# Moving the second layer's memory keys and values into the first layer, and three products and norm rows into another order

## The chip, the core and the metric

The kernel runs on one core of a Trainium2 chip. The metric is the device time of one execution in microseconds (us). TensorE (PE) multiplies matrices and loads its stationary operand (PEld) beside that, VectorE (DVE) and ScalarE (ACT) do elementwise work, GpSimd (POOL) does elementwise work and issues some DMAs, SyncE (SP) issues the weight loads.

## What is computed

The reference is a two-layer transformer block (`first_block`) and a second block with sparse attention and retention behind it. 512 tokens, width 1024, all in float32. Only the first block is touched by the change:

```python
mem_n = rmsnorm(mem, mem_norm)
for i in range(DEPTH):                       # DEPTH = 2
    if i == N_A:                             # layer 1 (called B)
        kv = rmsnorm(x, kv_norm) @ w_kv
        k, v = jnp.split(kv, 2, axis=-1)
        ...
    mem_kv = mem_n @ w_mem_kv[i]             # memory keys and values, 256 rows
    mk, mv = jnp.split(mem_kv, 2, axis=-1)
    h = rmsnorm(x, norm_mix[i])
    ...                                      # layer 0 (A): short convolution, layer 1 (B): band attention
    y_mem = _mem_attention(q_mem, mk, mv)
    x = x + jnp.concatenate([y_tok, y_mem], axis=-1) @ w_out
    h = rmsnorm(x, norm_ffn[i])
    x = x + (jax.nn.silu(h @ w_gate[i]) * (h @ w_up[i])) @ w_down[i]
```

The memory rows `mem_n` are the same in both layers; only the weights `w_mem_kv[i]` differ.

## The kernel before

Activations lie transposed: 8 chunks of 128 features by 512 tokens. A float32 product is made of three PE products of rounded parts (high by high, low by high, high by low: lines 120 to 122, or 142 to 144 for token-major results, or 575 to 577 in the feed-forward). A weight unit is 512 KB: SP loads it into `wr` (2 buffers), ACT rounds it to `wh` (line 70), DVE subtracts to get `wl` (line 80; 3 buffers each). One unit of 128 output features feeds 24 products (8 chunks by 3).

The program runs: `load_consts`, `layer_a`, `ffn(0)`, `layer_b`, `ffn(1)`, `second`. The framework fixes the order of each engine's instructions when it builds the program: an engine is given, of the instructions that its estimate holds ready, the one that stands earliest in the program text. Buffers of one tag (`b`, `t`, `s`, `x`, PSUM banks `pp`, `lg`, `tp`, `po`) are given out in text order and come back when the last reader is done. On the chip each engine then runs its list strictly in order.

The places that the change touches:

- `layer_a` (line 479): conv blocks 0 and 1, then `mem_kv(0)`, the memory queries and attention, conv blocks 2 to 5, then `residual`. A conv block is three weight units; its DVE results go through POOL (products `v` and `y`, line 73), then ACT and DVE.
- `mem_rows` (line 350) loads `mem` (1 MB), sums squares, makes the norm of the memory rows (`token_mean` at 174, `rsqrt`, `spread` at 203 to 207 into `mR`), and splits the gained rows into `gm` (8 chunks, tag `v`). `mem_kv` (372) multiplies them: two key units, two value units, 24 products of 256 columns each.
- `run` passes `between` to `ffn(0)`: there, before the last eight down products, `bias_loads`, `mem_kv(1)` (which loads and splits `mem` again) and `bias_tables` (which writes the 2.3 MB band table in DRAM) are called.
- `gate_up` (566): seven block products into the banks U, Y and Z; U is copied out by ACT (`g1`, `g2`, `u`) between its products; `between(0)` and `between(1)` insert down products of the group before. It is used from f = `PLAIN` = 5 on.
- `layer_b` (673): `hk` (8 chunks gained for keys), the norm (`square_sum`, `token_mean`, `rsqrt`, `spread` into `Rb`), `h` (8 chunks gained for queries), saving of x to DRAM (`xres`), then the two key products (`w_kv_k`), the values (`w_kv_v`), memory attention, band attention.

Of the kernel before, what the change touches and what calls it, by code (L numbers as in the profile page):

```python
# [9 lines left out]
F32R = mybir.dt.float32r  # L10
# [15 lines left out]
PLAIN = 5  # L26


class Build:
# [319 lines left out]
    def mem_rows(self):  # L349

        nc, T = self.nc, self.T
        chunks = []
        for i in range(4):
            t = self.slot("q", name="mem").rearrange("p (c n) -> p c n", c=2)
            nc.sync.dma_start(t, T["mem"][:, 2 * i:2 * i + 2])
            chunks += [t[:, 0], t[:, 1]]
        if self.mrs is None:
            acc = self.square_sum(chunks, 256, True, tags=("pa", "pa"))
            self.mrs = self.keep(self.rsqrt(self.token_mean(acc, 256, 1e-5, 1024.0)), "mrs")
            self.mR = self.spread(self.mrs, "mR")  # L360
        g = self.gain(5)
        res = []
        for c, x in enumerate(chunks):
            if c % 2 == 0:
                t = self.slot("v", F32R, (128, KWORDS), "gm")
            hi, lo = (t[:, a:a + 256] for a in (512 * (c % 2), 512 * (c % 2) + 256))
            self.copy(hi, x, g[:, c:c + 1])
            self.lo_of(lo, x, hi, g[:, c:c + 1])
            res.append((hi, lo))
        return res  # L370

    def mem_kv(self, layer):
        nc, T = self.nc, self.T
        gm = self.mem_rows()
        ks = []
        for b in range(2):
            ps = self.psum("lg")[:, :256]
            self.proj(ps, T["w_mem_k"][layer, b], gm)
            kk = self.slot("t", name="mk")[:, :256]
            self.mul(kk, ps, self.mR)  # L380
            ks += self.stack_k(kk, True)
        vs = []

        def done(tb, ps):
            hl = [self.slot("b", F32R, name="mv")[:, :384] for _ in range(2)]
            for t in hl:
                nc.gpsimd.memset(t.bitcast(F32), 0.0)
            hi, lo = (t.rearrange("p (i c) -> p i c", i=2) for t in hl)
            for i in range(2):
                for o in range(2):  # L390
                    src = ps[:, 128 * i + 64 * o:128 * i + 64 * o + 64]
                    d = slice(128 * o, 128 * o + 64)
                    self.copy(hi[:, i, d], src, self.mrs[:, tb:tb + 1])
                    self.lo_of(lo[:, i, d], src, hi[:, i, d], self.mrs[:, tb:tb + 1])
            vs.append(hl)

        self.proj_tok(T["w_mem_v"][layer], gm, 256, 2, done, tag=("tp",) if layer else ("lg",))
        return ks, vs

    def mem_attention(self, qs, ks, vs):  # L400

# [77 lines left out]
    def layer_a(self):  # L479
        nc, T = self.nc, self.T  # L480
        h = self.h0 + self.gained(self.x[1:], self.gain(0)[:, 1:])
        _, R = self.norm_row(1e-5, "Ra", True)
        ys = [self.conv_block(0, h, R, "b", self.w0)]
        ys.append(self.conv_block(1, h, R, "b", banks=("lg", "lg", "po")))
        ks, vs = self.mem_kv(0)
        qs = []
        for b in range(2):
            qs += self.stack_q(self.queries(T["a_w_in"][18 + b], h, R))
        ym = self.mem_attention(qs, ks, vs)
        for c in range(2, 6):  # L490
            ys.append(self.conv_block(c, h, R, "pb"))
        self.residual(T["a_w_out"], ys + ym)

    def halves(self, x, R, gain):
# [68 lines left out]
        put_sum("s4", s2, a12)  # L563
        return res

    def gate_up(self, src, B, between):

        nc, w = self.nc, self.pair_weights(src)
        mm = nc.tensor.matmul
        b11, b21, m1, m2, t3, b22, m4 = B  # L570

        def product(ps, a, b, start):
            for j in range(4):
                (ah, al), (bh, bl) = (a[0][:, j], a[1][:, j]), b[j]
                mm(ps, ah, bh, start=start and j == 0, stop=False, skip_group_check=not start)  # L575
                mm(ps, ah, bl, start=False, stop=False, skip_group_check=not start)  # L576
                mm(ps, al, bh, start=False, stop=j == 3, skip_group_check=not start)  # L577

        U, Y, Z = (self.psum(t)[:, :256] for t in ("pp", "lg", "lg"))
        g, u = self.slot("t", name="g"), self.slot("t", name="u")[:, :256]  # L580
        g1, g2 = g[:, :256], g[:, 256:]
        add = lambda out, a, b: nc.vector.tensor_tensor(out, a, b, op=ALU.add)  # L582
        product(U, w["a11"], b11, True)
        self.copy(g1, U)
        product(Y, w["a12"], b21, True)
        add(g1, Y, g1)
        product(U, w["s2"], m2, False)
        self.copy(g2, U)
        product(Z, w["s1"], m1, True)
        product(U, w["s3"], t3, False)  # L590
        self.copy(u, U)
        add(u, Z, u)
        between(0)
        product(Z, w["s4"], b22, False)
        add(g2, Z, g2)
        nc.scalar.activation(g, g, AF.Silu)  # L596
        product(U, w["a22"], m4, False)
        between(1)
        act = self.slot("t", name="act")
        self.mul(act[:, :256], U, g1)  # L600
        self.mul(act[:, 256:], u, g2)
        return self.split(act, "b", name="act")
# [14 lines left out]
        self.mul(u, u, z, self.nc.gpsimd)  # L617
        return self.split(u, "b", name="act"), R

    def ffn(self, layer, between_last=None):  # L620
        nc, T = self.nc, self.T
        gain = self.gain(2 + layer)
        h = self.gained(self.x, gain)
        R = B = act = None
# [17 lines left out]
        for g, (f0, f1) in enumerate(FFG):  # L642
            last = act
            todo = [] if last is None else [p for i in range(4) for p in down(i, last, g - 1)]
            act = []
            n = f1 - f0
            shares = [0] * n if last is None else [4, 2, 1, 1] if f0 < PLAIN else [8 * (i + 1) // n - 8 * i // n for i in range(n)]
            for f, share in zip(range(f0, f1), shares):
                mine, todo = todo[:share], todo[share:]

                def between(i):
                    for p in mine[i * (len(mine) // 2):] if i else mine[:len(mine) // 2]:
                        p()

                if f < PLAIN:
                    a, R = self.plain_gate_up(layer, f, h, R)
                    if f == 0:
                        steps = self.halves(self.x, R, gain)
                    sets = next(steps, None) or sets
                    between(0)  # L660
                    between(1)
                else:
                    if f == PLAIN:
                        B = [[s[i] for s in sets] for i in range(7)]
                    a = self.gate_up(T["w_gu"][layer, f - PLAIN], B, between)
                act.append(a)
        if between_last:
            between_last()
        for i in range(4):
            for p in down(i, act, len(FFG) - 1):  # L670
                p()
# [1 line left out]
    def layer_b(self):  # L673
        nc, T = self.nc, self.T
        hk = self.gained(self.x, self.gain(4), ["pa"] * 3 + ["pb"] * 5)
        rs, R = self.norm_row(1e-5, "Rb", True)
        rs = self.keep(rs, "rsb")
        h = self.gained(self.x, self.gain(1))
        xd = self.dr.tile([8, 128, 512], F32, name="xres")
        for c in range(8):  # L680
            nc.gpsimd.dma_start(xd[c], self.x[c])
        ks = []
        for b in range(2):
            ps = self.psum("pp")
            self.proj(ps, T["w_kv_k"][b], hk)
            kk = self.slot("t", name="k")
            self.mul(kk, ps, R)
            ks += self.stack_k(kk, tag="x")
        vs = []

        def done(tb, ps):
# [4 lines left out]
                vs.append(self.last_value(ps, rs[:, 3:]))  # L696

        self.proj_tok(T["w_kv_v"], hk, 256, 4, done, tag=("pp", "lg"))
        mk, mv = self.mem1
        qs = []  # L700
        for b in range(2):
            qs += self.stack_q(self.queries(T["b_w_q"][6 + b], h, R))
# [456 lines left out]

    def run(self):  # L1160
        self.load_consts()
        self.mrs = None
        self.layer_a()
        def between():
            loaded = self.bias_loads()
            self.mem1 = self.mem_kv(1)
            self.bias_tables(loaded)

        self.ffn(0, between)
        self.layer_b()  # L1170
        self.ffn(1)
        self.second()
# [123 lines left out]
```

## Time and profile before

| | us |
|---|---|
| median of 3 runs | 1663.72 (1663.45 to 1664.67) |
| the profiled execution | 1665.43 |
| its span, first to last instruction | 1663.6 |
| PE busy in the span | 1617.0 (97%) |
| PEld busy | 1415.1 (85%) |
| DVE busy | 1238.1 (74%) |
| ACT busy | 763.1 (46%) |
| POOL busy | 162.7 (10%) |

The profiled execution took 1.8 us beside its span and 1.7 us more than the median. PE is busy in nearly all of the span, but the end of a product is modelled and products overlap, so that busy time alone does not tell how fast PE runs: the distance from the start of one product to the start of the next does. A row of a timeline gives the start, the duration, the engine, the line, the operation, what it writes and reads, and in brackets how long the engine stood idle before it and what it waited for.

### The profile page before, as it was taken

The numbers are of one execution on the slowest core, as the hardware profiler recorded it, in microseconds if no ns is written. First come the engines' busy times: TensorE is split into PE (matmuls) and PEld (weight loads), VectorE is DVE, ScalarE is ACT, GpSimd is POOL, SyncE is SP. The second block draws the span as 40 slices with busy tenths as digits, with TensorE's granted clock in tenths as the row PEclk, the third lists the DMA queues.
The fourth block names the chain that finished last, engine by engine and source line by source line (L and its number), as shares of the span: only waits on it lengthen the run. The fifth ranks groups of instructions, "written<-read, shape, count | busy, mean of one in ns | idle before, by whom it ended". The sixth has DMA issues, their size and how long they took to land.

```text
span 1663.6 us, 24425 instructions
## 1 busy us (share of the span) xinstructions
PE 1617.0 (97%) x9408; PEld 1415.1 (85%) x9408; DVE 1238.1 (74%) x2342; ACT 763.1 (46%) x1418; POOL 162.7 (10%) x160
## 2 busy tenths in 40 slices
PE   8999999999999899999999999998999999999997
PEld 6887888999998688888899999987888888888887
DVE  7865787778776869978876877698788877764443
ACT  6532254445444557734444444444465533333333
POOL 1112410000000200051000000111001000010010
PEclk9999999999999899999999999999999999999999
DMA  6222223333323532222333333343501122243342
GB/s 201 89 85 93 92 86 101 115 93 94 117 90 118 197 107 64 78 94 76 114 102 98 93 102 104 89 166 98 163 26 58 45 83 83 71 152 115 126 160 88
DMA packets 51573, 171.61 MB, mean 103 GB/s; under 512 B 6680, under 2 KB 6880, under 8 KB 51328
## 3 DMA queue, kind: packets, MB, share of 16 engines
q1 hardware_dynamic: 45504, 151.11, 28.1%
q0 software_dynamic: 5376, 18.82, 3.4%
q8 instruction: 74, 1.21, 0.3%
q14 instruction: 43, 0.35, 0.1%
q10 hardware_dynamic: 576, 0.11, 0.0%
HBM read 160.56 MB, written 11.81 MB: 104 GB/s over the span
## 4 chain that ended last, share of the span: by engine, by line
PE 75%; DVE 12%; DMA 5%; issue 3%; ACT 3%; POOL 1%; SPq 0%; DVEq 0%; ACTq 0%; POOLq 0%
PE pp L122 8%; PE pp L120 8%; PE pp L121 8%; PE lg L120 4%; PE lg L121 4%; PE lg L122 4%; PE pp L575 3%; DMA wr<-in_w_gu_dram 3%; PE pp L576 3%; PE pp L577 3%; PE tp L120 3%; DVE wl L80 3%; PE tp L121 3%; PE tp L122 3%; PE tp L262 2%
## 5 line engine op out<-in xcount | busy, mean ns | idle before, releaser
L70 ACT ACTIVATE wh<-wr 128x1024 fp32r<-128x1024 f32 (+3 forms) x246 | 251.8, 1024 | 353.0 <-PE pp L121 130.3
L80 DVE TENSOR_TENSOR wl<-wr,wh 128x1024 fp32r<-128x1024 f32 (+3 forms) x246 | 305.3, 1242 | 53.8 <-ACT wh L70 52.5
L120 PE MATMUL pp<-g,wh 128*128 128x512 f32 x592 | 234.8, 397 | 8.5 <-ACT wh L70 8.0
L122 PE MATMUL pp<-g,wl 128*128 128x512 f32 x592 | 234.4, 396 | 0.6 <-DVE wl L80 0.6
L121 PE MATMUL pp<-g,wh 128*128 128x512 f32 x592 | 233.5, 394 | 0.0
L120 PEld LDWEIGHTS pp<-g,wh 128*128 128x128 f32 x592 | 112.0, 189 | 30.9 <-ACT wh L70 8.8
L122 PEld LDWEIGHTS pp<-g,wl 128*128 128x128 f32 x592 | 111.7, 189 | 22.6 <-DVE wl L80 1.5
L121 PEld LDWEIGHTS pp<-g,wh 128*128 128x128 f32 x592 | 111.9, 189 | 20.8 <-DVE g L76 0.6
L70 ACT ACTIVATE s<-s 128x512 fp32r<-128x512 f32 x136 | 84.8, 631 | 45.0 <-DVE s L555 42.9
L120 PE MATMUL tp<-acth,wh 128*128 128x512 f32 x264 | 103.8, 393 | 0.5 <-DVE mv L76 0.5
L121 PE MATMUL tp<-actl,wh 128*128 128x512 f32 x264 | 103.5, 392 | 0.0
L122 PE MATMUL tp<-acth,wl 128*128 128x512 f32 x264 | 102.8, 389 | 0.0
L80 DVE TENSOR_TENSOR s<-s,s 128x512 fp32r<-128x512 f32 x136 | 90.5, 684 | 0.3
L575 PE MATMUL pp<-Bh,s 128*128 128x256 f32 x272 | 79.0, 291 | 5.0 <-ACT g L70 4.8
L577 PE MATMUL pp<-Bh,s 128*128 128x256 f32 x272 | 78.0, 287 | 0.0
L575 PE MATMUL lg<-Bh,s 128*128 128x256 f32 x272 | 77.1, 283 | 0.0
L555 DVE TENSOR_TENSOR s<-wr,wr 128x512 f32<-128x512 f32 x68 | 46.8, 688 | 40.6 <-DMA wr<-in_w_gu_dram 40.2
L577 PE MATMUL lg<-Bh,s 128*128 128x256 f32 x272 | 76.9, 283 | 0.0
L596 ACT ACTIVATE g<-g 128x512 f32<-128x512 f32 x34 | 21.5, 632 | 83.3 <-DVE g L582 83.3
L122 PEld LDWEIGHTS tp<-acth,wl 128*128 128x128 f32 x264 | 49.7, 188 | 10.8
L575 PEld LDWEIGHTS pp<-Bh,s 128*128 128x128 f32 x272 | 53.0, 195 | 6.8 <-ACT g L70 6.6
L576 PE MATMUL pp<-Bl,s 128*128 128x256 f32 x204 | 58.5, 287 | 0.0
(503 smaller groups left out, 4546.6 us busy)
## 6 DMA issues: line engine op xcount, KB each, us to landing
wr<-in_w_gu_dram SPq DMA_DIRECT2D x68, 512.0 KB, 3.9
wr<-in_w_in_dram SPq DMA_DIRECT2D x44, 512.0 KB, 3.5
wr<-in_w_down_dram SPq DMA_DIRECT2D x32, 512.0 KB, 3.6
wr<-in_a_w_in_dram SPq DMA_DIRECT2D x18, 512.0 KB, 3.5
wr<-in_w_down_dram SPq DMA_DIRECT2D x16, 384.0 KB, 3.2
wr<-in_w_gate_dram SPq DMA_DIRECT2D x10, 512.0 KB, 3.4
wr<-in_w_up_dram SPq DMA_DIRECT2D x10, 512.0 KB, 3.4
wr<-in_a_w_out_dram SPq DMA_DIRECT2D x8, 512.0 KB, 3.4
```

The lines of the kernel that those rows point to most:

```text
L70: self.nc.scalar.activation(out, in_, AF.Copy, scale=scale)
L80: self.nc.vector.tensor_tensor(out, x, hi.bitcast(F32), op=ALU.subtract)
L120: mm(ps, ah, bh, start=start, stop=False)
L121: mm(ps, ah, bl, start=False, stop=False)
L122: mm(ps, al, bh, start=False, stop=stop)
L262: self.nc.tensor.transpose(ps[:, c:c + 128], src, self.ident)
L555: nc.vector.tensor_tensor(t, a, b, op=ALU.add)
L575: mm(ps, ah, bh, start=start and j == 0, stop=False, skip_group_check=not start)
L576: mm(ps, ah, bl, start=False, stop=False, skip_group_check=not start)
L577: mm(ps, al, bh, start=False, stop=j == 3, skip_group_check=not start)
L596: nc.scalar.activation(g, g, AF.Silu)
```

## The change

`mem_rows` returns the sum of squares; the norm of the memory rows is made in `mem_kv(0)` behind the first key product. `mem_kv(1)` runs in layer A behind conv block 3 from the same `gm`; its keys and values go to DRAM (`set_aside`, 12 stores on the POOL queue) and come back in layer B (`bring_back`, 8 loads on the POOL queue). The band table is made behind conv block 4. In `gate_up` for f = 5 the first inserted down product stands ahead of the `s2` product and no longer behind `u`. In `layer_b` the norm sum stands behind the first key product and the norm row behind the second; `h` and the saving of x follow them.

```diff
-        if self.mrs is None:
-            acc = self.square_sum(chunks, 256, True, tags=("pa", "pa"))
-            self.mrs = self.keep(self.rsqrt(self.token_mean(acc, 256, 1e-5, 1024.0)), "mrs")
-            self.mR = self.spread(self.mrs, "mR")
+        acc = self.square_sum(chunks, 256, True, tags=("pa", "pa"))
...
-    def mem_kv(self, layer):
+    def mem_kv(self, layer, gm, acc=None):
...
             self.proj(ps, T["w_mem_k"][layer, b], gm)
+            if acc is not None and b == 0:
+                self.mrs = self.keep(self.rsqrt(self.token_mean(acc, 256, 1e-5, 1024.0)), "mrs")
+                self.mR = self.spread(self.mrs, "mR")
...
+    def set_aside(self, ks, vs):
+        self.aside = [self.dr.tile([128, n], F32R, name=f"aside{i}") for i, n in enumerate([512] * 4 + [384] * 4)]
+        for d, k in zip(self.aside, ks):
+            for i in range(2):
+                self.nc.gpsimd.dma_start(d[:, 256 * i:256 * i + 256], k[i])
+        for d, t in zip(self.aside[4:], [t for v in vs for t in v]):
+            self.nc.gpsimd.dma_start(d, t)
+
+    def bring_back(self):
+        ts = []
+        for d in self.aside:
+            n = d.shape[1]
+            t = self.slot("b", F32R, name="mk")[:, :n]
+            self.nc.gpsimd.dma_start(t, d)
+            ts.append(t)
+        return [(t[:, :256], t[:, 256:]) for t in ts[:4]], [ts[4:6], ts[6:8]]
...
-        ks, vs = self.mem_kv(0)
+        gm, acc = self.mem_rows()
+        ks, vs = self.mem_kv(0, gm, acc)
...
         for c in range(2, 6):
             ys.append(self.conv_block(c, h, R, "pb"))
+            if c == 2:
+                loaded = self.bias_loads()
+            if c == 3:
+                self.set_aside(*self.mem_kv(1, gm))
+            if c == 4:
+                self.bias_tables(loaded)
...
         add(g1, Y, g1)
+        if first:
+            between(0)
         product(U, w["s2"], m2, False)
...
         add(u, Z, u)
-        between(0)
+        if not first:
+            between(0)
...
-                    a = self.gate_up(T["w_gu"][layer, f - PLAIN], B, between)
+                    a = self.gate_up(T["w_gu"][layer, f - PLAIN], B, between, f == PLAIN)
...
-        if between_last:
-            between_last()
...
         hk = self.gained(self.x, self.gain(4), ["pa"] * 3 + ["pb"] * 5)
-        rs, R = self.norm_row(1e-5, "Rb", True)
-        rs = self.keep(rs, "rsb")
+        acc = self.square_sum(self.x, first=True)
+        ps = [self.psum("pp") for _ in range(2)]
+        self.proj(ps[0], T["w_kv_k"][0], hk)
+        rs = self.keep(self.rsqrt(self.token_mean(acc, 512, 1e-5, 1024.0)), "rsb")
+        self.proj(ps[1], T["w_kv_k"][1], hk)
+        R = self.spread(rs, "Rb")
+        kk = [self.slot("t", name="k") for _ in range(2)]
+        for b in range(2):
+            self.mul(kk[b], ps[b], R)
         h = self.gained(self.x, self.gain(1))
...
-        ks = []
-        for b in range(2):
-            ps = self.psum("pp")
-            self.proj(ps, T["w_kv_k"][b], hk)
-            kk = self.slot("t", name="k")
-            self.mul(kk, ps, R)
-            ks += self.stack_k(kk, tag="x")
+        ks = [k for x in kk for k in self.stack_k(x, tag="x")]
...
-        mk, mv = self.mem1
+        mk, mv = self.bring_back()
```

## Rows read from the trace of the kernel before

**Rows 1.** The page, part 1: busy us, share of the span, instructions.
```profile
PE 1617.0 (97%) x9408; PEld 1415.1 (85%) x9408; DVE 1238.1 (74%) x2342; ACT 763.1 (46%) x1418; POOL 162.7 (10%) x160
```
**Rows 2.** Stretches: length, busy time (instructions) per engine, PEclk, DMA share, GB/s.
```profile
204.00:265.00 61.00, 60.80 (x267) 49.65 (x267) 52.76 (x92) 28.14 (x42) 8.63 (x5) 1.00 0.27 86
265.00:280.00 15.00, 12.86 (x82) 12.04 (x81) 10.79 (x17) 6.50 (x11) 0.00 (x0) 0.89 0.38 115
528.00:552.00 24.00, 19.40 (x126) 16.34 (x125) 17.93 (x35) 14.17 (x29) 7.20 (x11) 1.00 0.45 132
571.00:592.00 21.00, 15.53 (x57) 12.17 (x56) 15.47 (x35) 7.17 (x11) 2.69 (x4) 0.76 0.47 147
815.00:830.00 15.00, 12.76 (x83) 12.00 (x82) 11.11 (x18) 6.50 (x11) 0.00 (x0) 0.89 0.35 117
```
**Rows 3.** Timeline of ACT in layer A: two roundings of weight units, one unit apart.
```profile
109.23 1.06 ACT L70 ACTIVATE wh<-wr 128x1024 fp32r<-128x1024 f32 x1 [2.44 <-PE pp L121]
114.67 1.06 ACT L70 ACTIVATE wh<-wr 128x1024 fp32r<-128x1024 f32 x1 [4.38 <-PE pp L121]
```
**Rows 4.** Timeline of PE from the memory products to the values of layer B.
```profile
530.41 0.28 PE L120 MATMUL lg<-gm,wh 128*128 128x256 f32 x1
530.52 0.28 PE L121 MATMUL lg<-gm,wh 128*128 128x256 f32 x1
...
545.57 0.81 PE L333 MATMUL po<-s,m 32*12 32x384 f32 x2
...
570.68 0.39 PE L120 MATMUL pp<-gh,wh 128*128 128x512 f32 x1
...
592.40 0.28 PE L142 MATMUL pp<-wh,gh 128*128 128x256 f32 x1
```
**Rows 5.** Timeline of PE: the two waits at the start of layer B.
```profile
574.37 1.86 PE L174 MATMUL tp<-ones,acc 128*128 128x2 f32 x8 [2.62 <-DVE acc L166]
579.08 0.79 PE L122 MATMUL pp<-gh,wl 128*128 128x512 f32 x1 [2.85 <-DVE wl L80]
```
**Rows 6.** Timeline of PE: the norm at the start of `second`.
```profile
1106.61 1.84 PE L174 MATMUL tp<-ones,acc 128*128 128x2 f32 x16
1108.31 0.48 PE L120 MATMUL pp<-g,wh 128*128 128x512 f32 x1
...
1113.65 1.02 PE L206 MATMUL tp<-dg,ones 128*128 128x512 f32 x2
1114.11 0.80 PE L122 MATMUL pp<-g,wl 128*128 128x512 f32 x1
...
1116.09 0.50 PE L120 MATMUL pp<-g,wh 128*128 128x512 f32 x1 [0.48 <-DVE f L73]
```
**Rows 7.** Timeline of PE and ACT in `gate_up` of `ffn(0)`, f = 5.
```profile
273.26 0.44 PE L575 MATMUL pp<-Bh,s 128*128 128x256 f32 x1 [2.14 <-ACT g L70]
...
275.85 0.63 PE L120 MATMUL tp<-acth,wh 128*128 128x512 f32 x1
```
**Rows 8.** Timeline of ACT in the same stretch.
```profile
272.31 0.63 ACT L70 ACTIVATE a<-wr 128x512 fp32r<-128x512 f32 x1 [1.50 <-DMA wr<-in_w_gu_dram]
272.84 0.37 ACT L70 ACTIVATE g<-pp 128x256 f32<-128x256 f32 x1
...
274.30 0.63 ACT L70 ACTIVATE s<-s 128x512 fp32r<-128x512 f32 x1 [0.57 <-DVE s L555]
```
**Rows 9.** Timeline of PE and DVE in `mem_kv(0)`: the norm of the memory rows.
```profile
55.12 1.22 PE L206 MATMUL tp<-dg,ones 128*128 128x256 f32 x2 [2.46 <-DVE dg L203]
```
**Rows 10.** Timeline of DVE in the same stretch.
```profile
50.56 0.69 DVE L80 TENSOR_TENSOR yl<-y,yh 128x512 fp32r<-128x512 f32 x1 [1.85 <-ACT yh L70]
```
**Rows 11.** DMA issues between 540 and 600: queue, KB each, median us to landing.
```profile
band<-band POOLq DMA_DIRECT2D x1, 2304.0 KB, 12.3
xres<-x POOLq DMA_DIRECT2D x8, 256.0 KB, 5.6
...
wr<-in_w_kv_k_dram SPq DMA_DIRECT2D x2, 512.0 KB, 9.7
```
**Rows 12.** Timeline of POOL: two table loads of `second` into tag `b`.
```profile
1079.81 1.15 POOL L923 DMA_DIRECT2D nrope<-in_nrope_dram  x2
```

More of the change, by code (lines that the diff above doesn't have):

```diff
@@ L369, in mem_rows @@
             res.append((hi, lo))
-        return res
-    def mem_kv(self, layer):
+        return res, acc
+    def mem_kv(self, layer, gm, acc=None):
         nc, T = self.nc, self.T
-        gm = self.mem_rows()
         ks = []
@@ L395, in done @@
             vs.append(hl)
-        self.proj_tok(T["w_mem_v"][layer], gm, 256, 2, done, tag=("tp",) if layer else ("lg",))
+        self.proj_tok(T["w_mem_v"][layer], gm, 256, 2, done, tag=("lg",))
         return ks, vs
+    def set_aside(self, ks, vs):
[13 more added lines that the diff above has]
+        return [(t[:, :256], t[:, 256:]) for t in ts[:4]], [ts[4:6], ts[6:8]]
     def mem_attention(self, qs, ks, vs):
@@ L564, in pair_weights, with gate_up @@
         return res
-    def gate_up(self, src, B, between):
+    def gate_up(self, src, B, between, first):
         nc, w = self.nc, self.pair_weights(src)
@@ L618, in plain_gate_up, with ffn @@
         return self.split(u, "b", name="act"), R
-    def ffn(self, layer, between_last=None):
+    def ffn(self, layer):
         nc, T = self.nc, self.T
@@ L1161, in run @@
         self.load_consts()
-        self.mrs = None
         self.layer_a()
[L1164 to L1169, printed above, removed]
+        self.ffn(0)
         self.layer_b()
```

## The prediction

> **What bounds the kernel now.** I read the shares first. PE is busy for 97% of the span and no other engine is near it [rows 1], so an edit pays only where it shortens PE's list or takes a hole out of it. This change takes no product away: the memory products of layer B are moved, not dropped. So the question is which holes go and which come.
>
> The second view is the table of stretches [rows 2]. 204 to 265 is what an undisturbed stretch looks like: PE 60.80 us of 61, clock 1.00. The other four rows have the holes: idle 2.14 us (265 to 280) and 2.24 us (815 to 830), both at a mean clock of 0.89; idle 4.60 us (528 to 552); idle 5.47 us at a clock of 0.76 (571 to 592). A fifth hole is one wait of 2.46 us in layer A [rows 9]. All five lie where the change works.
>
> Idle time alone undercounts a hole, because the products behind it can run at half rate. So I count work instead. Two prices: a unit of 24 products of 512 columns lasts 114.67 - 109.23 = 5.44 us, 0.227 us a product [rows 3]; a product of 256 columns comes every 0.12 us (530.52 - 530.41, rounded up) [rows 4].
>
> - *End of ffn(0).* From the first memory product (530.41) to the first key product of layer B (570.68) are 40.27 us [rows 4]. In it lie 96 memory products (11.5 us), the band table's two (0.8) and 96 down products (21.8): 34.1. Lost: 6.2 us.
> - *Start of layer B.* From 570.68 to the first value product (592.40) are 21.72 us [rows 4]. In it lie 48 products (10.9), eight norm sums (16 took 1.70, so 0.85) and the spread (0.46, and 0.41 on the product behind it) [rows 6]: 12.6. Lost: 9.1 us. Two waits of 2.62 and 2.85 make most of it [rows 5], half-rate products the rest.
> - *gate_up, f = 5, twice.* The wait is 2.14; then 12 products take 275.85 - 273.26 = 2.59 us where 12 x 0.12 = 1.44 is the usual, and the next two are 0.2 late each [rows 7]. With the idle step's own edges (about 0.15) 3.8 us, and about the same at 815 [rows 2]. Lost: 7.6 us.
> - *Memory norm in layer A.* 2.5 us [rows 9].
>
> Together 25.4 us: what the change could win at the very most.
>
> **The change part by part.**
>
> *End of ffn(0), 6.2 us lost.* The memory products, the second load of `mem` (4 DMAs), the second split into `gm` (8 on ACT, 8 on DVE) and the band table leave; last down products follow the last gate product directly. ffn(1) ends in just that way, and from 1106.61 backwards the trace shows no wait: the first bracket is that of 1116.09 [rows 6]. Cover for the last activation's split: the inserted down product and the first three quarters of the next. I take all 6.2 (5 to 6.2).
>
> *Start of layer B, 9.1 us lost.* In the old text `h` (8 bulky splits) stands ahead of the key weights, and DVE reaches `wl` only after them: the wait of 2.85 [rows 5]. In the new text `wl` comes first and nothing of the norm stands ahead of the first key product. The first unit (5.4 us) covers the last chunk's gain and the sum; the second covers rsqrt. DVE also loses the memory work it carried into this stage, and the weights no longer share the DMA engines with the band table: they took 9.7 us to land there [rows 11]. What is late next: both `pp` banks are held until `Rb` is there. In `second`, which has the same order (two products in `pp`, sum, spread), PE waits 0.48 for that [rows 6]. There the sum runs amid the first unit; here it stands behind it, so up to 2 us more of rsqrt is uncovered. I leave 1.9 us (0.5 to 4). Gain 7.2 (5 to 8.6). The xres stores now queue on POOL behind eight loads (0.57 us of POOL each [rows 12], 4.6 us), and the stacked keys, which take over x's buffers, wait for them; band attention needs those more than 40 us later. Nothing else waits there.
>
> The Trainium skill (Perfetto Trace Analysis, Identifying the Most-Contended Engine) calls matmul busy time a bad measure of how near TensorE is to its limit and wants the busy share of weight loads. By that measure the healthy stretch has 49.65 / 61 = 0.81 and 571 to 592 has 0.58, so that its hole would be 21 - 12.17 / 0.81 = 6.0 us instead of PE's idle 5.5; counting products gives 9.1 [rows 2, 4]. The trace agrees that busy PE hides loss, but the share of loads hides most of it too; the sum by it would start from about 22 us.
>
> *gate_up, 7.6 us lost.* PE waits for ACT's copy `g`, which stands on ACT behind the split of the next f's `a`, and that waits for its weights until 272.31 [rows 8]. That landing hangs on DVE and on `wr`, not on PE, so it stays. One inserted down product (12 x 0.227 = 2.7 us) in front gives PE work across the old wait of 2.14. But `g` becomes ready 2.7 us later, and ACT's list is fixed: the split `s` that begins at 274.30, 2.0 us behind `a` [rows 8], is then the earlier of the two. `g` would end near 275.3 while PE is there at 273.7. So I leave 1.6 us of wait and some half rate: about 2.1 of 3.8, twice. Gain 3.4 (0 to 7). Behind `u` PE loses the filler that hid copy and add (about 0.4 us each); the second inserted down product is ready there and takes its place, 1 us each if not.
>
> *Memory norm, 2.5 us lost.* The sum moves behind the first key unit (24 x 0.12 = 2.9 us later), the spread about as far down PE's list. DVE's chain started late not for the sum but for `yl`, which waits 1.85 for conv block 1's POOL product [rows 10]; it starts hardly later now. Cover: one half of the value products. I leave 1.0 (0 to 2.5). Gain 1.5.
>
> *mem_kv(1) in layer A.* The same 96 products (11.5 us) cost the same there. Their four weight units are wanted every 2.9 us where conv units are wanted every 5.4, but up to three split units and two raw ones can be ahead when they begin; DVE needs about 11 us for this part, about what PE takes. No row shows this place, so bounds: nothing (behind 56 us `mem_kv(0)` runs with no bracket), and the 4.6 us of idle that the same work cost at 528 [rows 2]. I take 0.6, near the first, since conv blocks leave the split ahead as in [rows 3].
>
> *DRAM trip.* 12 stores hold POOL about 12 x 0.57 = 7 us [rows 12]. Queued behind them are conv block 4's POOL products, wanted 11 us after the last memory product. Zero; if they came later than that, a microsecond each. The eight loads go to tag `b`; such a load is issued as soon as earlier `b` tiles are handed out: the tables of `second` were issued at 1079.81, at the end of ffn(1) [rows 12]. So they leave some 20 us ahead of layer B; at 5.6 us a store beside the band copy [rows 11] they are back long before memory attention. Zero. The band table's copy takes 12.3 us and slows loads to 9.7 [rows 11]; two are in flight, 4.9 us a unit, under the 5.44 that PE needs. Zero (0 to 2).
>
> **Sum.** 6.2 + 7.2 + 3.4 + 1.5 - 0.6 = 17.7 us. The profiled execution took 1665.4 (span 1663.6 and 1.8 around it): 1647.7 for one like it, and 1.7 less for the median: 1646.0.
>
> **Rivals.**
> - *The stalls of gate_up and of the memory norm only move* (ACT's list puts still more ahead of `g`; DVE's chain ends as late as PE's new place for the spread). For: both ends are fixed by DMA and POOL, not PE. Against: PE has 2.7 and 2.9 us more to do before it gets there. Time: 1646.0 + 3.4 + 1.5 = 1650.9.
> - *The norm chain of layer B is drawn out.* Its 14 small DVE steps let a bulky one (0.7 to 1.2 us) in between each two, as wherever weight splits are ready; ten of them put the spread some 6 us behind the second key product with both banks held, and half-rate products follow. Then the 7.2 do not come: 1653.
> - *The orders hardly change*: each engine's list is made from estimates, and only the move of the memory work shows. 6.2 - 0.6 is left: 1658.
> - *All holes close*: 25.4 less the spread's bank wait of about 1 in layer B: 1640.
> - *Slower: the DMA engines are crowded in layer A.* 1.8 MB of stores and the band copy (2.3 MB read and written) now meet the weight loads of conv 4, conv 5 and the residual. It decides from the point at which weight loads stand still longer than PE's store of two split and two arriving units, 4 x 5.44 = 22 us; each microsecond beyond costs one. To outweigh 17.7 they must stand for over 40 us; 46 would give 1670. Against: [rows 11] show loads that still land in 9.7 under the same copy and eight stores.
>
> **How the numbers follow.** Chances: forecast 0.54, stalls move 0.17, chain drawn out 0.12, orders hardly change 0.05, all close 0.08, crowded 0.04. The likeliest is 1646. 1639 to 1656 takes in all but the last and most of the fourth. A measurement can tell about 0.2% (3.3 us) from no change; all cases but the last are beyond it on the fast side, though worse ends of two together come near: faster 0.93, same 0.03, slower 0.04.
>
> **What would show it.** Right: no bracket on PE from the last gate product of ffn(0) to the last down product; key products of layer B at 0.227 us with at most 2 us of waits ahead of the values; at f = 5 a wait under 2 us; no bracket on memory products behind conv block 3. Wrong: PE brackets on `wl` or `wh` between conv 3 and the residual (crowding), `dg` far behind the second key product (chain), a bracket on `g` over 2 us (moved). Wrong altogether, if PE's holes elsewhere grow because all lists are made anew.

## The result, and the profile after

The changed kernel took 1652.78 us (median of 4 executions, 1649.6 to 1654.58) beside 1663.59 for the kernel before: a ratio of 0.9936, 95% interval 0.9925 to 0.9948. The gain is 10.8 us. The forecast was 1646.0, a gain of 17.7, with 1639 to 1656 as its range.

The profiled execution took 1654.55 (span 1652.8). First the page: the span, and busy time with its share and count for each engine.

```profile
span 1652.8 us, 24455 instructions
PE 1614.7 (98%) x9408; PEld 1412.1 (85%) x9408; DVE 1235.1 (75%) x2334; ACT 760.9 (46%) x1410; POOL 173.9 (11%) x180
```

PE has the same 9408 products as before; ACT and DVE have 8 instructions less each, POOL has 20 more for the trip through DRAM [rows 1]. The spans differ by 10.8 us: PE's idle time fell from 46.6 to 38.1 us and its busy time by 2.3. Second, the table of stretches after (length, busy time and count of PE, PEld, DVE, ACT, POOL, then PEclk, DMA share, GB/s):

```profile
120.00:140.00 20.00, 20.00 (x135) 18.51 (x134) 14.21 (x25) 10.80 (x21) 9.20 (x15) 1.00 0.69 193
160.00:180.00 20.00, 17.83 (x71) 14.06 (x70) 10.76 (x11) 4.42 (x5) 4.65 (x3) 0.91 0.59 183
280.00:300.00 20.00, 17.85 (x111) 16.09 (x110) 13.51 (x22) 7.41 (x13) 0.00 (x0) 0.93 0.41 132
540.00:560.00 20.00, 20.00 (x110) 17.38 (x109) 12.61 (x19) 10.01 (x15) 10.07 (x15) 1.00 0.57 186
560.00:580.00 20.00, 20.00 (x94) 16.67 (x93) 19.25 (x31) 13.26 (x20) 4.17 (x7) 1.00 0.53 178
```

The two holes around 528 to 592 [rows 2] are closed: PE is busy for 40.00 us of 40 from 540 to 580, at a clock of 1.00. The memory work in its new place, 120 to 140, runs without a hole too. But f = 5 (280 to 300) still has one, and 160 to 180, at the start of layer A's residual, has a new one. Third, the brackets of over 0.25 us on PE between 25 and 600 us, in order of time:

```profile
57.12 0.70 PE L206 MATMUL tp<-dg,ones 128*128 128x256 f32 x2 [2.45 <-DVE dg L203]
171.69 0.50 PE L120 MATMUL pp<-yh,wh 128*128 128x512 f32 x1 [1.33 <-ACT yh L70]
173.03 0.50 PE L121 MATMUL pp<-yl,wh 128*128 128x512 f32 x1 [0.84 <-DVE yl L80]
291.20 0.39 PE L600 MATMUL pp<-Bh,s 128*128 128x256 f32 x1 [0.40 <-ACT g L70]
294.93 0.39 PE L600 MATMUL pp<-Bh,wh 128*128 128x256 f32 x1 [1.34 <-ACT u L70]
296.08 0.39 PE L600 MATMUL lg<-Bh,s 128*128 128x256 f32 x1 [0.41 <-DVE u L607]
526.15 0.39 PE L600 MATMUL pp<-Bh,s 128*128 128x256 f32 x1 [1.16 <-ACT g L70]
```

The memory norm waits 2.45 where it waited 2.46 [rows 9]. At f = 5 the wait on `g` fell from 2.14 [rows 7] to 0.40, and two on `u` came. The two at 171.69 and 173.03 are larger than at the same place of before:

```profile
156.88 0.49 PE L120 MATMUL pp<-yh,wh 128*128 128x512 f32 x1 [0.59 <-ACT yh L70]
157.60 0.50 PE L121 MATMUL pp<-yl,wh 128*128 128x512 f32 x1 [0.23 <-DVE yl L80]
```

To weigh places I add up, over a stretch, how much later each product starts behind the one ahead than products of its shape and line usually do (the lower quartile of these distances); this is called "lost" below. What counts as usual is a choice, so a place's sum is good to about half a microsecond, and a sum over the whole span is not given. For the two profiled executions:

| place | lost before | lost after |
|---|---|---|
| first 25 us | 5.3 | 6.9 |
| memory norm, 45 to 70 | 4.6 | 4.7 |
| start of layer A's residual | 1.5 | 4.7 |
| f = 5 of ffn(0) | 5.1 | 4.7 |
| end of ffn(0), start of layer B | 16.4 | 2.8 |

In the fifth row, 1.3 of the 2.8 are the wait at f = 21 (526.15); the end of ffn(0) and layer B proper have 1.5 left, of which 0.9 is the spread itself.

### The profile page after: what moved, and what is told of

Read it like the earlier page. It is cut to its first block, busy times and chain, and to the rows that moved or that the text cites. A ratio compares the mean times of both kernels' runs of the same rounds, so it can differ in the third digit from the quotient of the medians.

```text
span 1652.8 us, 24455 instructions
## 1 busy us (share of the span) xinstructions
PE 1614.7 (98%) x9408; PEld 1412.1 (85%) x9408; DVE 1235.1 (75%) x2334; ACT 760.9 (46%) x1410; POOL 173.9 (11%) x180
## 4 chain that ended last, share of the span: by engine, by line
PE 75%; DVE 13%; DMA 6%; ACT 3%; issue 2%; POOL 0%; DVEq 0%; SPq 0%; ACTq 0%; POOLq 0%
PE pp L121 8%; PE pp L122 8%; PE pp L120 8%; DMA wr<-in_w_gu_dram 4%; PE lg L120 4%; PE lg L121 4%; PE lg L122 4%; PE pp L600 3%; DVE wl L80 3%; PE pp L601 3%; PE pp L602 3%; PE tp L120 3%; PE tp L121 3%; PE tp L122 2%; PE tp L262 2%
## 5 line engine op out<-in xcount | busy, mean ns | idle before, releaser
L248 POOL MEMSET v<- 128x1152 f32 x8 | 8.3, 1061 | 540.6 <-PE lg L602 540.6
L601 PE MATMUL lg<-Bl,s 128*128 128x256 f32 x204 | 57.8, 283 | 0.0
```

The source lines that it names most:

```text
L248: self.nc.gpsimd.memset(v.bitcast(F32), 0.0)
```

## The experiments

Each group of runs was timed against the kernel before on the same chip; that kernel's own median moved between groups from 1658.4 to 1664.8 us, so ratios are compared and not times.

| kernel | ratio to before | 95% interval |
|---|---|---|
| order_only | 0.9970 | 0.9959 to 0.9981 |
| mem_only | 0.9926 | 0.9909 to 0.9944 |
| gate_undo | 0.9917 | 0.9902 to 0.9933 |
| band_late | 0.9914 | 0.9897 to 0.9930 |
| band_only | 1.0028 | 1.0018 to 1.0039 |
| mem_band | 0.9930 | 0.9918 to 0.9943 |
| norm_y | 0.9928 | 0.9915 to 0.9942 |
| after_again (the changed kernel) | 0.9934 | 0.9921 to 0.9946 |
| three_gate | 0.9920 | 0.9904 to 0.9936 |
| three | 0.9918 | 0.9901 to 0.9935 |
| four | 0.9911 | 0.9896 to 0.9926 |
| five | 0.9876 | 0.9858 to 0.9895 |

**Who closed the hole of layer B?** The prediction gave its 7.2 us to the new order of the norm. Two kernels take the change apart: order_only is the kernel before with the new text of `layer_b`; mem_only is the changed kernel with the old text of `layer_b` and of `gate_up`.

```diff
# order_only, against the kernel before: the new layer_b as in the change, but
-        mk, mv = self.bring_back()
+        mk, mv = self.mem1
```
```diff
# mem_only, against the changed kernel: the old layer_b, but
-        mk, mv = self.mem1
+        mk, mv = self.bring_back()
```

> The kernel before with the new text of layer B alone (key weights first, norm sum behind the first key product, spread behind the second); the memory work stays between the last activation and the last down products of ffn(0). If the hole at the start of layer B came of the order of the norm, 7 to 9 us go: 1655 to 1657, and the waits of 2.62 and 2.85 us on PE are gone. If it came of the memory work in front, which loads DVE and the DMA engines (weights took 9.7 us to land there), the order gives 0 to 3 us: 1661 to 1664, with PE waiting for `wh` or `wl` of the key weights. The hole inside the memory work, 6.2 us, stays in either case.

> The changed kernel with the old text of layer B and the old order of gate_up: the moved memory work and the moved memory norm alone. By a sum of places: 6.2 us at the end of ffn(0) less 2.9 lost ahead of the residual of layer A, 1660.3. If the hole at the start of layer B hung on the memory work, part of its 9.1 us goes here too: 1652 to 1657. If neither place gains alone, 1663.

The order alone gained 5.0 us (0.0030 x 1664.8), the moved memory work alone 12.3. Both together, which is gate_undo below, gained 13.8. The order gained an amount between its two expectations, the move more than any of its three; with the move made, the order adds 1.5 us, inside the intervals. They are two cures for one hole, and the move alone is enough. In mem_only PE's timeline shows why: first key product, last one ahead of the norm sum, and the norm sum (8 small products):

```profile
564.30 0.39 PE L120 MATMUL pp<-gh,wh 128*128 128x512 f32 x1
...
567.70 0.39 PE L120 MATMUL pp<-gh,wh 128*128 128x512 f32 x1
567.93 0.95 PE L174 MATMUL tp<-ones,acc 128*128 128x2 f32 x8
```

The sum starts 567.93 - 564.30 = 3.63 us behind the first key product, with no bracket. In the kernel before it started 574.37 - 570.68 = 3.69 us behind it [rows 4, 5]. DVE's last `acc`, and its `wl` of the first key weights, first in before and then in mem_only:

```profile
573.62 0.69 DVE L166 TENSOR_TENSOR acc<-acc,sq 128x512 f32<-128x512 f32 x1
577.81 1.22 DVE L80 TENSOR_TENSOR wl<-wr,wh 128x1024 fp32r<-128x1024 f32 x1
```
```profile
567.04 0.68 DVE L166 TENSOR_TENSOR acc<-acc,sq 128x512 f32<-128x512 f32 x1
560.74 1.22 DVE L80 TENSOR_TENSOR wl<-wr,wh 128x1024 fp32r<-128x1024 f32 x1
```

`acc` ends 3.63 us behind the first key product in before and 3.42 in mem_only, so it is as late in both. But mem_only's list on PE has 16 key products ahead of the sum, and that of before had 4, so that PE had to wait 2.62. The second wait, of 2.85, goes in the same way: DVE's list has `wl` 3.6 us ahead of the first key product, where before had it 7.1 us behind. The text of this stretch is the same in both kernels. The likely reason is that the builder orders each list by its estimate of what is ready, and that the memory work in front changed the estimate; no trace shows the estimate itself.

In order_only the sum stands behind all 24 key products and PE still waits, since now the key weights come late (ACT, DVE, PE):

```profile
564.92 1.06 ACT L70 ACTIVATE wh<-wr 128x1024 fp32r<-128x1024 f32 x1 [2.92 <-DMA wr<-in_w_kv_k_dram]
566.01 1.23 DVE L80 TENSOR_TENSOR wl<-wr,wh 128x1024 fp32r<-128x1024 f32 x1 [2.77 <-ACT wh L70]
579.41 1.68 PE L174 MATMUL tp<-ones,acc 128*128 128x2 f32 x8 [1.13 <-DVE acc L166]
```

DVE stands still for 2.77 us behind a weight that has not landed, and `acc`, which stands further down its list, ends 7.62 us behind the first key product instead of 3.63. The band copy is in flight then, so the next two kernels moved the band table by itself: band_only is the kernel before with the table built in ffn(0) behind f = 2, mem_band is mem_only with the table back at its old place. The edit of band_only (here, and wherever the table goes to ffn(0), its one-hot rows also take the `sa` buffer):

```diff
-            loaded = self.bias_loads()
             self.mem1 = self.mem_kv(1)
-            self.bias_tables(loaded)
...
                 act.append(a)
+                if layer == 0 and f == 1:
+                    loaded = self.bias_loads()
+                if layer == 0 and f == 2:
+                    self.bias_tables(loaded)
```

and that of mem_band, against mem_only:

```diff
-            if c == 2:
-                loaded = self.bias_loads()
...
-            if c == 4:
-                self.bias_tables(loaded)
...
+        if layer == 0:
+            self.bias_tables(self.bias_loads())
         for i in range(4):
             for p in down(i, act, len(FFG) - 1):
```

> The kernel before with one thing moved: the loads and the copy of the band table go to behind f = 1 and f = 2 of ffn(0); the memory work stays at the end of ffn(0), the text of layer B is the old one. Moving the memory work alone closed the hole at the start of layer B too, with the old text of layer B. If it was the band copy (12.3 us, key weights landing in 9.7 us, their `wl` on DVE at 577.81) that made that hole, it closes here as well: 7 to 10 us less than before, about 1655. If it was the memory work's own share of DVE and ACT, the hole stays (9 us), and only the table's two products (0.8 us) and some waits inside the memory work go: 1661 to 1664.

> The other corner: the memory work in layer A, old order of layer B and of gate_up, but the loads and the copy of the band table back between the last activation and the last down products of ffn(0). If the copy made the hole of layer B, it is back: 5 to 9 us slower than the same kernel with the table in layer A, 1656 to 1660, with PE waiting on the key weights' `wh` or `wl`. If the memory work made it, the time stays within 1.5 us of that kernel, or gains 1 to 2 us, since the loads of `a_w_out` in layer A no longer meet the copy: 1649 to 1652.

In band_only the hole of layer B is there to the hundredth:

```profile
573.87 1.41 PE L174 MATMUL tp<-ones,acc 128*128 128x2 f32 x8 [2.62 <-DVE acc L166]
578.12 0.80 PE L122 MATMUL pp<-gh,wl 128*128 128x512 f32 x1 [2.85 <-DVE wl L80]
```

Same brackets as in [rows 5] without the copy: the hole of before is one of list order, not of DMA. The kernel was even 0.28% slower than before; the cause stays open. In mem_band the copy at the end of ffn(0) costs something again: one wait of 1.93 on `acc`, 5.6 us lost at the end of ffn(0) and the start of layer B against 2.0 in mem_only. It wins 1.7 at layer A's residual and 2.0 at f = 5, and the ratios agree. So of the two, the memory work made the hole; the copy costs some 2 to 4 us wherever it meets weights.

**What holds the start of layer A's residual?** band_late is the changed kernel with the band table moved to ffn(0), as in band_only.

> The changed kernel with the loads and the copy of the band table moved out of layer A, to behind f = 1 and f = 2 of ffn(0). If that copy (2304 KB, 11.8 us) is what held the first `a_w_out` load and so `wh` and the last conv block's `yh` on ACT, the two waits of 1.33 and 0.84 us at the start of the residual and the half rate behind them go: 2 to 3 us faster than the changed kernel, about 1650, unless the copy now holds weights of ffn(0) in their place (then a bracket on `wh` at 215 to 235 us, and no gain). If the last block's own chain over POOL made the wait, it stays within 0.3 us, and the time with it.

In the changed kernel (SP, POOL, ACT) the load, the copy, and what stands behind the load:

```profile
158.56 0.33 SPq L111 DMA_DIRECT2D wr<-in_a_w_out_dram  x1
157.47 0.56 POOL L340 DMA_DIRECT2D band<-band  x1 [2.75 <-DMA band<-s]
170.06 1.06 ACT L70 ACTIVATE wh<-wr 128x1024 fp32r<-128x1024 f32 x1 [7.62 <-DMA wr<-in_a_w_out_dram]
171.02 0.61 ACT L70 ACTIVATE yh<-y 128x512 fp32r<-128x512 f32 x1
```

The load was issued 1.1 us behind the copy and landed 11.4 us later, 0.7 us behind the end of the copy; the median of this matrix's loads is 3.8, and 3.4 in band_late. POOL had `y` ready at 167.76 + 1.30 = 169.06, but on ACT `yh` stands behind the `wh` that waits for the load: 2 us late. In band_late ACT's two are

```profile
165.12 1.06 ACT L70 ACTIVATE wh<-wr 128x1024 fp32r<-128x1024 f32 x1 [4.33 <-PE lg L121]
167.50 0.63 ACT L70 ACTIVATE yh<-y 128x512 fp32r<-128x512 f32 x1 [1.32 <-POOL y L73]
```

and 0.7 us are lost there instead of 4.7. The cause is shown. But the kernel gained only what the interval can hardly tell (0.9914 against 0.9934 to 0.9936), since the copy now ran from 253.9 on and met the first `w_down` and `w_gu` loads (not at 215 to 235, where the expectation looked for that): 7.5 us lost around f = 5 against 4.7.

**What is the edit in gate_up worth?** gate_undo is the changed kernel without it.

```diff
-                    a = self.gate_up(T["w_gu"][layer, f - PLAIN], B, between, f == PLAIN)
+                    a = self.gate_up(T["w_gu"][layer, f - PLAIN], B, between, False)
```

> The changed kernel with the order inside gate_up put back: at f = 5 the inserted down product stands behind `u` again. The traces of before and after say that the wait on `g` only changed place (lost between 260 and 300 us: 4.6 us before, 4.5 after; at the second layer's f = 5, 5.0 before, about 4.0 after): by this theory the kernel is 0 to 1.5 us slower than the changed one, PE's wait on `g` at f = 5 is back at about 2.1 us and the waits on `u` (1.3 us) are gone. The prediction's own term, 3.4 us, would make it 3 to 4 us slower than the changed kernel (about 1656), with something else having eaten as much elsewhere. Below the changed kernel's time by over 1 us: the new order costs more than it saves.

> The changed kernel once more, beside the other three on the same chip, so that 1 to 3 us between them and it can be told: by its first times about 0.994 of the kernel before.

0.9917 against 0.9936, and 0.9934 when the changed kernel ran once more (after_again): not slower, if anything faster. At f = 5 the wait on `g` is back, those of 1.34 and 0.41 are gone, and 3.6 us are lost against 4.7:

```profile
287.53 0.39 PE L600 MATMUL pp<-Bh,s 128*128 128x256 f32 x1 [2.06 <-ACT g L70]
```

At f = 5 of ffn(1) it is the other way round, 5.7 lost in gate_undo against 3.5, so that over both layers the edit is worth about 1 us by this count. What gate_undo gained lies elsewhere: at layer A's residual, which its edit doesn't touch, 1.9 us are lost against 4.7, with a first wait of 0.20 instead of 1.33. In the changed kernel ACT's list at f = 5 is this:

```profile
289.52 0.63 ACT L70 ACTIVATE a<-wr 128x512 fp32r<-128x512 f32 x1 [1.98 <-DMA wr<-in_w_gu_dram]
290.25 0.63 ACT L70 ACTIVATE s<-s 128x512 fp32r<-128x512 f32 x1
290.79 0.36 ACT L70 ACTIVATE g<-pp 128x256 f32<-128x256 f32 x1
292.71 1.89 ACT L70 ACTIVATE s<-s 128x512 fp32r<-128x512 f32 x3 [1.56 <-DVE s L579]
294.51 0.37 ACT L70 ACTIVATE u<-pp 128x256 f32<-128x256 f32 x1
```

`a` waits for the landing, three `s` wait for DVE's sums of what landed, and `u` stands behind them. PE waited 1.7 us less for `g` and met the same chain at `u`. The pair three_gate and three, timed together, differ in this edit alone: 0.9920 and 0.9918, 0.3 us apart where each interval has 2.7 us to either side. The 3.4 us of the prediction are not there.

**What holds the memory norm?** Two edits: norm_y takes conv block 1's last product from POOL to DVE; four (below) puts the spread behind the first half of the values.

```diff
-        self.mul(y, y, b, nc.gpsimd)
+        self.mul(y, y, b, None if c == 1 else nc.gpsimd)
```

> The changed kernel with the last product of conv block 1 (`y` times `b`) on DVE instead of POOL. DVE's list is fixed, and `yl` of that block stands ahead of the memory norm's chain; it waits 1.83 us for ACT's `yh`, and that for POOL's product of 2.13 us. If this is what ends the spread's wait of 2.45 us on PE, the chain starts 1 us earlier and the wait falls to 1 to 1.6 us, the kernel gains about 1 us. If the split `wl` inside the chain, which waits for ACT's `wh` and that for PE's first key unit, sets it, the wait stays at 2.2 to 2.5 us and the time with it.

The spread on PE and the split inside the chain on DVE, in norm_y:

```profile
52.94 1.23 DVE L80 TENSOR_TENSOR wl<-wr,wh 128x1024 fp32r<-128x1024 f32 x1
...
56.38 0.70 PE L206 MATMUL tp<-dg,ones 128*128 128x256 f32 x2 [1.89 <-DVE dg L203]
```

`yl` no longer waits for POOL, yet the wait fell only from 2.45 to 1.89: the `wl` of 1.23 us stands in the middle of the chain, and behind it are still eleven small steps. So both expectations were half right. The ratio, 0.9928 beside 0.9934 for the changed kernel, can't tell the gain. In three, which has this edit and no band loads in layer A, the wait was 1.34.

**A version that adds up what held.** three_gate is band_late with norm_y's edit; three is that with the old order in gate_up; four also places the spread later, and five builds the band table behind the memory queries of layer A (in buffers that are free there):

```diff
         def done(tb, ps):
+            if acc is not None and tb == 0:
+                self.mR = self.spread(self.mrs, "mR")
+                keys()
```
```diff
         ys = [self.conv_block(0, h, R, "b", self.w0)]
+        loaded = self.bias_loads()
...
             qs += self.stack_q(self.queries(T["a_w_in"][18 + b], h, R))
+        self.bias_tables(loaded)
```

> The changed kernel with two of the edits tried here together: the band table's loads and copy behind f = 1 and f = 2 of ffn(0), and the last product of conv block 1 on DVE. If places add up: 2 to 3 us off the start of layer A's residual and about 0.6 off the spread's wait, 0.992 of the kernel before against 0.9935 for the changed kernel. If the copy costs in ffn(0) what it saves in layer A: 0.9935.

> The same with the order inside gate_up put back. Beside three_gate it gives the price of that edit alone, under the same runs of before. Prediction's term: 3.4 us slower than three_gate. The stalls only move: within 1 us of it. New waits cost more than the old one: 1 to 2 us faster.

> The same as `three`, and the spread of the memory norm and the key products' scaling placed in the text behind the first half of the value products, so that PE has 16 products of 256 columns more (1.9 us) ahead of the spread. If that wait on `dg` is only a matter of PE's place, its 1.9 us go to under 0.4 and the kernel gains 1.5 us over `three`: 0.990 of before. If DVE's chain ends later with the new place (more bulky splits inside it), the wait stays and the time with it.

> The kernel `four` with the band table built in layer A behind the memory queries, so that its copy (2304 KB) runs during memory attention, where the DMA engines were busy for 0.16 (70 to 80 us) and 0.01 (80 to 90 us). Behind f = 2 of ffn(0) the copy slipped to 251 to 264 us and met the first `w_down` and `w_gu` loads; lost between 255 and 325 us: 8 to 9 us, against 5 without the copy there. If the copy costs only what it meets, 3 to 4 us go and nothing comes: 0.989 of before. If it holds the weights of conv 2 in layer A (a bracket on `wh` at 85 to 100 us), it costs there what it saves, 0.991.

In four no bracket is left on the spread; 1.2 us are lost from 45 to 70, against 2.2 in three and 4.7 in the changed kernel. The ratio, 0.9911, moved the way expected, inside the interval. In three and four the copy slipped to 250 us. A `w_down` load issued 0.1 us behind it took 4 us; the next, 1.2 us behind it, took 11.9 in three (first the copy's own row) and 12.6 in four:

```profile
band<-band POOLq DMA_DIRECT2D x1, 2304.0 KB, 12.7
wr<-in_w_down_dram SPq DMA_DIRECT2D x1, 512.0 KB, 11.9
```

and in four 9.1 us were lost around f = 5. In five the copy is issued at 74.61, in memory attention. From 74.7 to 86.2 the table of DMA queues has no row for SP's weights, only the copy's on POOL's queue (packets, MB, share of the engines' time):

```profile
q0 software_dynamic: 144, 2.36, 73.9%
band<-band POOLq DMA_DIRECT2D x1, 2304.0 KB, 11.7
```

The weight load before it landed at 73.05, the next was issued when it was over:

```profile
69.58 0.33 SPq L111 DMA_DIRECT2D wr<-in_a_w_in_dram  x1
86.36 0.33 SPq L111 DMA_DIRECT2D wr<-in_a_w_in_dram  x1
```

So the copy meets no weight. PE is busy for all of 70 to 90, 4.7 us are lost around f = 5, 0.7 at the residual. (The profiled execution, 1641.67, is the slowest of its four and only 2.3 us under that of four.) five is at 0.9876 of before (0.9858 to 0.9895), 20 us under it, and the fastest of all: below the changed kernel by 0.6%, with intervals that don't touch. These are ratios from two groups of runs; that of the changed kernel itself came out at 0.9936 and 0.9934 in its two.

## Why the prediction was right and wrong

The time fell into the range because terms that were too large and too small partly cancelled: three gave too much (gate_up, the memory norm, the band copy at zero), two too little (the start of layer B, the memory work in layer A). A range of 17 us left room for that, and 1652.78 alone would also have suited the rival of a drawn-out norm chain (1653), whose mechanism didn't show: layer B's spread begins at 582.78, 0.3 us behind the start of the last key product, without a bracket. By the steps of the sum, forecast gain and what the places of the two profiled executions show:

| step | forecast | found |
|---|---|---|
| end of ffn(0) | 6.2 | 6.2 |
| start of layer B | 7.2 | 9.0 |
| gate_up, both layers | 3.4 | 1.3 by place, 0 by the pair of runs |
| memory norm | 1.5 | 0 |
| memory work in layer A | -0.6 | 0 |
| band copy in layer A | 0 | -3.2 |
| first 25 us, f = 21 (not in the sum) | | -1.6, -1.3 |

With 1.3 for gate_up these add up to 10.4; the spans differ by 10.8.

*End of ffn(0)* held as worked out: no bracket on PE between 526.15 and the end of the key products.

*Start of layer B*: the size held, the owner did not. From the first key product (570.83) to the first value product (582.67) are 11.84 us; 48 products and the sums are 11.75 of them, so 0.1 is lost where 9.1 were. The prediction left 1.9 for the banks that wait for `Rb`; in fact the builder put a value product ahead of the spread, and PE didn't wait. What failed is the step that took the hole for one of the text's order ("In the old text `h` (8 bulky splits) stands ahead of the key weights"). mem_only shows that the old order, without the memory work in front, gets a list without the hole. The rival "the orders hardly change", that only the move of the memory work shows, was nearer in its mechanism; its 1658 was wrong since it kept the hole of layer B. The hole's size also tells the two ways of measuring it apart. The Trainium skill (Perfetto Trace Analysis, Identifying the Most-Contended Engine) names the busy share of weight loads as one of two better measures than busy matmuls; by it the hole would have been 6.0 us. Counting products gave 9.1, and 9.0 came back.

*gate_up*: the first half of the step held (the landing stays, `g` gets later by a little). The failing half is its end: "the second inserted down product is ready there and takes its place, 1 us each if not". What came at `u` was the chain of three `s`, waits of 1.34 and 0.41 us, in both layers. Here, and at the memory norm, the rival "the stalls only move" was the right one; it had 0.17.

*Memory norm*: the cover (one half of the value products) was counted, but the builder put the spread behind 8 value products and not 24, and DVE's chain took a bulky `wl` in. four, which also has norm_y's edit, shows that the cover would have done, had the text asked for it.

*Band copy*: put at zero because loads under the copy took 9.7 us [rows 11], 4.9 a unit with two in flight. That is a misreading of a median of two. Taken by themselves (windows 551 to 552 and 559 to 560), the two loads of before are

```profile
wr<-in_w_kv_k_dram SPq DMA_DIRECT2D x1, 512.0 KB, 11.7
wr<-in_w_kv_k_dram SPq DMA_DIRECT2D x1, 512.0 KB, 7.7
```

The first was in flight for 8 us before the second was issued, and landed at 562.96, 0.9 us behind the end of the copy. The load at layer A's residual did the same, took 11.4, and ACT's list let a finished `y` wait behind it. The price was 3.2 us in this execution and 1.2 in the next one of the same kernel (2.7 lost), where the clock did not fall. The bounds (0 to 2) were too narrow; the rival of crowded DMA engines had the mechanism and put its point of decision, 22 us of standing weights, far too high, since it counted PE's store of weights and not what else waits on ACT behind one.

*Memory work in layer A and the DRAM trip* cost nothing that a bracket shows: no bracket on PE from 120 to 152, with the DMA engines busy for 0.69 of 120 to 140, and none at layer B's memory attention.

The first 25 us, which the change doesn't touch, lost 5.3 to 7.8 us in the various kernels, and the wait at f = 21 was not there when the changed kernel ran again. Such differences are part of the spread of 1649.6 to 1654.58.

## What to carry to other kernels

Before a hole is credited to one edit, ask whether another part of the same change would close it as well: undoing one edit at a time shows that, and a sum of gains counts the hole twice or names the wrong owner. Where the builder orders each engine's list by estimate, look at how many products stand ahead of the waiting one rather than at the text. And a bulk copy that nobody waits for has a price set by its place: put it where no load will be issued until it is over. A median of two landings can hide that one of them waited for the copy: look at the loads one by one.

## What the runs showed of the hardware

A weight load that is issued behind this bulk copy from DRAM to DRAM lands when the copy is over. In 13 of the 14 profiled executions, those of before and after among them, a load of 512 KB was issued 0.5 to 2.9 us behind the copy. It took 10.3 to 13.0 us, where such loads usually take 3.4 to 3.8, and landed 0.2 to 1.3 us behind the end of the copy. In four of them another load was issued only 0.1 us behind the copy and took 4.0 to 4.2. The fourteenth is five, whose copy met no load and took 11.7 us, as long as beside one (11.8 in the changed kernel). The queue rows of the changed kernel from 158.9 to 164.7, when one load was in flight beside the copy (packets, MB, share of the engines' time; the copy is on POOL's queue q0, the weights on SP's q1):

```profile
q0 software_dynamic: 79, 1.46, 84.6%
q1 hardware_dynamic: 16, 0.07, 6.1%
```

The copy's packets are 1.46 MB / 79 = 18 KB, the load's 4 KB. The Trainium skill (DMA: Bandwidth & Descriptors, Queues, rings and completion order) says that an engine takes turns between its queues packet by packet; by that a weight load beside the copy would get 4 of 22, an estimate of a fifth of the bytes. The trace agrees in direction and not in size: as it counts packets, the load had 16 turns against 79, and a twentieth of the bytes (0.07 of 1.53 MB). So turns by packet alone don't explain the wait, and the rest of the cause stays open.

A slightly longer wait can cost far more than its length. At the residual the changed kernel waited 1.33 and 0.84 us in one profiled execution, 0.93 and 0.84 in the next. The stretches at and behind the second wait (columns as in the table of stretches):

```profile
173.00:177.00 4.00, 3.97 (x12) 3.14 (x13) 1.09 (x2) 1.45 (x2) 0.34 (x1) 0.64 0.38 131
```
```profile
171.00:175.00 4.00, 3.16 (x13) 2.39 (x14) 1.80 (x3) 0.71 (x1) 0.00 (x0) 1.00 0.36 131
```

In the first the granted clock fell to 0.64 on the mean, between its levels of 1.2 and 2.4 GHz, and products came every 0.43 us from 174.37 to 177.36. In the second it stayed at 1.00. The place lost 4.7 us in one and 2.7 in the other. Three more kernels have the copy at this place and the same second wait of 0.84. With a first wait of 1.38 (norm_y) the clock fell too, and 4.5 us were lost; with 0.64 (mem_only) and 0.20 (gate_undo) it did not, and 2.1 and 1.9 were. So up to 2.8 us between these kernels come from this place and not from the edits that they were made to test.
